# A diffusion backbone layer on one core: token pieces, paired modulation weights and a fixed TensorE order in the front

## The chip, the cores and the metric

The kernel runs on one core of a Trainium2 chip. The metric is the device time of one launch in microseconds (us), the median of three runs. A core has five engines that run side by side, each in its own order: TensorE (PE in the profile; PEld are its weight loads), VectorE (DVE), ScalarE (ACT), GpSimd (POOL) and SyncE (SP), which here issues nearly all transfers. SBUF is the memory that the engines work in, PSUM the eight banks that TensorE writes.

## The reference

One layer over 1024 latent tokens with 256 context tokens, width 1024. Cut to what matters here:

```python
mod_x = (jax.nn.silu(c) @ w_ada[i] + b_ada[i])[:, None, :]     # latent: six vectors of 1024
mod_c = jax.nn.silu(c_ctx) @ w_ada[i] + b_ada[i]               # context
sh1, sc1, g1, sh2, sc2, g2 = jnp.split(mod_x, 6, axis=-1)
csh1, csc1, ...            = jnp.split(mod_c, 6, axis=-1)
px = modulate(rms_norm(x, norm1_w[i]), sh1, sc1) @ w_in[i]     # modulate(h, s, c) = h * (1 + c) + s
pc = modulate(rms_norm(ctx, norm1_w[i]), csh1, csc1) @ w_in[i]
...  # columns of px, pc: gated DeltaNet (q, k, v with a short conv, z) and neighbourhood attention (q, k, v)
x = x + g1 * (concatenate([dn_x, na_x]) @ w_out[i])
x = x + g2 * swiglu(modulate(rms_norm(x, norm2_w[i]), sh2, sc2), w_ffn_in[i], w_ffn_out[i])
```

## The kernel before, in words

Everything is transposed: the width lies on the 128 partitions in eight tiles (`KT` = 8, index k), the 1280 tokens (256 of context, then 1024 latent) on the columns. `SEGS` cuts the columns into 256, 512 and 512, one PSUM bank each. For accuracy, each operand of a large product is split into a high part in fp32r and the rest: tokens into `hh` and `hl`, weights into `whi` and `wlo`, and a product is three: hh by whi, hh by wlo, hl by whi.

The front does this in order. The eight token tiles `xt` are loaded whole, then four of the eight tiles of the first modulation weights (`wada`), the raw weights of the first two blocks (`fraw`), and the other four. ACT squares each token tile, DVE adds the squares (`acc`), PE multiplies by ones (`m`), ACT takes a logarithm and an exponential: `rs`, the reciprocal norm of each token. `ada(q)` computes a fourth of the modulation: 16 products of weight tiles with the two conditioning vectors (`pm<-wada,wide`), a copy to the row `arow`, and four products that turn the row into columns (`pm<-sel,arow`), from which `mod1` (shift and scale) and `w1s` (norm weight times 1 + scale) are made. For each k, DVE scales `xt` by `w1s` and `rs`, ACT adds the shift and rounds (`hh`), DVE takes the rest (`hl`), and PE does the products of the first two blocks (`first`, key columns of the DeltaNet), six of the eight PSUM banks.

Behind that, one block of 128 output columns follows the other; a block's weights are cast by ACT and POOL (`load` in `weights`) into one of two buffers `whi`/`wlo`. The third block's weights are loaded early into the one raw buffer `wraw`, and cast when the buffer of the first block is free. DVE evacuates a block from PSUM while taking the taps of the convolution (`cacc`). A later job of another kind (`Wide`) has weight tiles of its own, `zhi` and `zlo`, in the pool `zp`.

What sets the order: the program is written as below, and a scheduler that simulates the engines puts the instructions of each engine in order, so products of different k and parts of `ada` can change places. Tiles wait for the last reader of the memory that they reuse.

Of the kernel before, what the change touches and what calls it, by code (L numbers as in the profile page):

```python
# [9 lines left out]
F32 = mybir.dt.float32  # L10
# [77 lines left out]
def hybrid(ctx, tc, a, dbg):  # L88
    nc = tc.nc
    pe, act, dve, pool, sp = nc.tensor, nc.scalar, nc.vector, nc.gpsimd, nc.sync  # L90
# [97 lines left out]
    def weights(wp, raws=2):  # L188
        def load(src, kt=KT, n=128, lo_engine=pool, raw=None):
# [3 lines left out]
            hi = wp.tile([128, KT, 128], F32R, name="whi", tag="whi")  # L193
            lo = wp.tile([128, KT, 128], F32R, name="wlo", tag="wlo")
# [159 lines left out]
    with ExitStack() as bs:  # L354
# [31 lines left out]
        class Block:  # L386
# [7 lines left out]
            def prefetch(self, raw=None):  # L394
# [3 lines left out]
                self.w = load_w(src, raw=raw)  # L398
# [205 lines left out]
        with ExitStack() as xs:  # L604
# [13 lines left out]
            for k in range(KT):  # L618
                x = xp.tile([128, T], F32, name=f"xt{k}", tag=f"xt{k}")
                sp.dma_start(x, a["xcT"][k])  # L620
                xt.append(x)
            for j in range(4):
                load_ada(j)
            raws = [xp.tile([128, KT, 128], F32, name=f"fraw{i}", tag=f"fraw{i}") for i in range(2)]
            for i in range(2):
                sp.dma_start(raws[i], a["w_conv"][4 + i])
            for j in range(4, 8):
                load_ada(j)
# [8 lines left out]
            def ada(q):  # L637
# [8 lines left out]
                (act.copy if q else dve.tensor_copy)(row, p)  # L646
                p = bank("pm")
                for b in range(4):
                    pe.matmul(p[:, 2 * b:2 * b + 2], row[:, b * 128:(b + 1) * 128], sel, start=True, stop=True)
                b0 = 4 * (q // 2) + 8 * (1 - q % 2)  # L650
                if q % 2:
                    for b in range(4):
                        act.activation(mod1[:, b0 + b], p[:, 2 * b:2 * b + 2], AF.Identity,
                                       bias=bada[:, b0 + b:b0 + b + 1])
                else:
                    dve.tensor_tensor(mod1[:, b0:b0 + 4], p[:, 0:8].rearrange("p (b c) -> p b c", c=2),
                                      bada[:, b0:b0 + 4].rearrange("p (b c) -> p b c", c=1).to_broadcast([128, 4, 2]),
                                      OP.add)
                    b = b0 - 8
                    dve.scalar_tensor_tensor(w1s[:, b:b + 4], mod1[:, b0:b0 + 4], 1.0,  # L660
# [3 lines left out]
            for k in range(KT):  # L664
                sq = xp.tile([128, T], F32, name="sq", tag="sq", bufs=2)
                act.activation(sq if k else acc, xt[k], AF.Square)
                if k:
                    dve.tensor_tensor(acc, acc, sq, OP.add)
# [9 lines left out]
            for k in range(KT):  # L678
# [11 lines left out]
                for b in first:  # L690
                    b.mm([k], (0, 2), 1)
# [1009 lines left out]
```

## Time and profile before

| what | us |
|---|---|
| median of three runs | 1558.21 |
| runs, lowest to highest | 1553.05 to 1559.2 |
| profiled execution | 1560.1 |
| its span in the trace | 1558.3 |
| PE busy in the span | 1469.4 (94%) |
| DVE busy | 1002.2 (64%) |
| ACT busy | 715.9 (46%) |
| POOL busy | 189.7 (12%) |

Times of the trace count from the span's start. A timeline row gives the start, the time from the first instruction's start to the last one's end, engine, line, operation, output and inputs, shape, count, and in brackets the idle time of the engine before it with what ended it. A group row gives total busy time and the mean in ns. In the view of stretches each row gives the busy time of PE, PEld, DVE, ACT and POOL in one stretch, then the granted clock of TensorE (1.00 is full), the share of the transfer engines and GB/s.

### The profile page before, as it was taken

How to read it: one execution, taken by the hardware profiler on the slowest of the kernel's cores; microseconds unless marked ns; L12 is line 12 of the kernel's file. 1: busy time of each engine (PE TensorE's matmuls, PEld its weight loads, DVE VectorE, ACT ScalarE, POOL GpSimd, SP SyncE). 2: the span in 40 equal slices, each digit the busy share in tenths (PEclk: the TensorE clock that was granted, in tenths of full speed). 3: DMA queues.
4: the chain of work that ended last, by engine and by line, in shares of the span. 5: the costliest groups of instructions: out<-in, count | busy, mean ns of one | idle time of the engine just before them, and what ended most of it. 6: DMA issues, size and time to landing. Idle time of an engine off the chain costs nothing.

```text
span 1558.3 us, 23894 instructions
## 1 busy us (share of the span) xinstructions
PE 1469.4 (94%) x8535; PEld 1226.4 (79%) x8535; DVE 1002.2 (64%) x1905; ACT 715.9 (46%) x1404; POOL 189.7 (12%) x255
## 2 busy tenths in 40 slices
PE   3999998999999989998898989999999999999998
PEld 1789777777978868887777878888888888888887
DVE  4866479345264665778886479755555656689652
ACT  5333362594356446556663175333333334444441
POOL 1043610342143300000110000000000000000000
PEclk9999999999999999999999999999999999999999
DMA  9457123554478489998627603523332234698742
GB/s 368 135 165 246 58 74 120 205 178 142 147 220 253 143 249 287 281 260 239 204 77 262 217 34 108 183 102 102 102 102 101 102 102 150 233 375 295 236 155 81
DMA packets 208455, 276.30 MB, mean 177 GB/s; under 512 B 16128, under 2 KB 115024, under 8 KB 207312
## 3 DMA queue, kind: packets, MB, share of 16 engines
q1 hardware_dynamic: 207472, 274.15, 54.7%
q8 instruction: 67, 1.10, 0.3%
q10 hardware_dynamic: 864, 0.63, 0.1%
q14 instruction: 52, 0.43, 0.1%
HBM read 209.93 MB, written 68.98 MB: 179 GB/s over the span
## 4 chain that ended last, share of the span: by engine, by line
PE 48%; DVE 2%; ACT 1%; DMA 0%; issue 0%; SPq 0%; ACTq 0%; DVEq 0%
PE ps L1267 27%; PE ps L1620 13%; PE ps L1404 3%; PE ps L1426 1%; PE sc L318 1%; PE sc L308 1%; PE sc L1210 1%; PE sc L1386 0%; DMA wraw<-w_out 0%; DVE x L1459 0%; PE ps L1134 0%; DVE bt L298 0%; PE sc L296 0%; PE ps L1103 0%; PE ps L1113 0%; PE ps L1122 0%
## 5 line engine op out<-in xcount | busy, mean ns | idle before, releaser
L383 PE MATMUL blk<-hh,whi 128*128 128x512 f32 (+1 forms) x416 | 126.8, 400 | 9.7 <-ACT zt L585 5.6
L1328 ACT CAST uhi<-ws 128x512 fp32r<-128x512 f32 x91 | 54.7, 622 | 150.5 <-PE ps L1267 71.7
L1328 ACT CAST uhi<-wq 128x512 fp32r<-128x512 f32 x101 | 60.6, 621 | 134.3 <-issue 58.0
L383 PE MATMUL blk<-hh,wlo 128*128 128x512 f32 (+1 forms) x416 | 119.7, 384 | 2.3 <-POOL wlo L199 2.3
L383 PE MATMUL blk<-hl,whi 128*128 128x512 f32 (+1 forms) x416 | 116.6, 379 | 0.0
L1329 DVE TENSOR_TENSOR ulo<-wq,uhi 128x512 fp32r<-128x512 f32 x101 | 67.4, 687 | 67.4 <-ACT uhi L1328 37.2
L1267 PE MATMUL ps<-hT,uhi 128*128 128x512 f32 x336 | 104.1, 391 | 3.1 <-ACT hT L1452 3.1
L1267 PE MATMUL ps<-lT,uhi 128*128 128x512 f32 x336 | 103.9, 391 | 0.0
L1267 PE MATMUL ps<-hT,ulo 128*128 128x512 f32 x336 | 103.6, 389 | 0.0
L383 PEld LDWEIGHTS blk<-hh,whi 128*128 128x128 f32 x416 | 71.5, 198 | 25.9 <-ACT zt L585 6.0
L383 PEld LDWEIGHTS blk<-hh,wlo 128*128 128x128 f32 x416 | 75.8, 199 | 19.4 <-POOL wlo L199 2.8
L1267 PE MATMUL ps<-hB,uhi 128*128 128x512 f32 x288 | 89.7, 392 | 0.0
L1267 PE MATMUL ps<-lB,uhi 128*128 128x512 f32 x288 | 89.2, 391 | 0.0
L1267 PE MATMUL ps<-hB,ulo 128*128 128x512 f32 x288 | 88.9, 389 | 0.0
L383 PEld LDWEIGHTS blk<-hl,whi 128*128 128x128 f32 x416 | 74.4, 194 | 14.1
L574 PE MATMUL blk<-zhi,hh 128*128 128x264 f32 (+1 forms) x288 | 85.4, 296 | 0.0
L1329 DVE TENSOR_TENSOR ulo<-ws,uhi 128x512 fp32r<-128x512 f32 x91 | 60.8, 686 | 36.4 <-ACT uhi L1328 28.1
L574 PE MATMUL blk<-zhi,hl 128*128 128x264 f32 (+1 forms) x288 | 82.8, 287 | 0.0
L574 PE MATMUL blk<-zlo,hh 128*128 128x264 f32 (+1 forms) x288 | 82.4, 286 | 0.0
L1267 PEld LDWEIGHTS ps<-hT,uhi 128*128 128x128 f32 x336 | 62.9, 188 | 16.6 <-ACT hT L1452 3.5
L1267 PEld LDWEIGHTS ps<-hT,ulo 128*128 128x128 f32 x336 | 63.3, 189 | 13.2
L1267 PEld LDWEIGHTS ps<-lT,uhi 128*128 128x128 f32 x336 | 63.4, 189 | 13.2
(341 smaller groups left out, 3539.3 us busy)
## 6 DMA issues: line engine op xcount, KB each, us to landing
wq<-w_fo SPq DMA_DIRECT2D x99, 256.0 KB
wq<-w_gu SPq DMA_DIRECT2D x88, 256.0 KB
wad<-wa SPq DMA_DIRECT2D x64, 256.0 KB
bt<-rpb SPq DMA_DIRECT2D x64, 192.0 KB
t_d<-g SPq DMA_DIRECT2D x22, 512.0 KB
fr<-t_d SPq DMA_DIRECT2D x44, 256.0 KB
f_d<-g SPq DMA_DIRECT2D x33, 256.0 KB
fr<-f_d SPq DMA_DIRECT2D x33, 256.0 KB
```

Of the source, the lines that this page charges most:

```text
L308: pe.transpose(sc[:, u * 640 + j * 128:u * 640 + (j + 1) * 128], bt[:, j * 128:(j + 1) * 128], ident)
L318: pe.matmul(sc[u * ND:u * ND + ND, 1280:1408], vv, pt[:, j * 128:(j + 1) * 128], start=j == 0, stop=j == 4)
L383: pe.matmul(o, ww[:, k], xx[k][:, s], start=k == 0 and j == 0, stop=k == KT - 1 and j == end)
L574: pe.matmul(p[:, :c1 - c0], x[k][:, s], ww[:, k, c0:c1], start=k == 0 and j == 0, stop=k == KT - 1 and j == 2)
L1210: pe.matmul(o, w[wi][:, k], parts[xi][4 + k][:, t], start=k == 0 and j == 0, stop=False, skip_group_check=True)
L1267: pe.matmul(o, w[wi][:, k], x[xi][:, k], start=first and k == 0 and j == 0, stop=k == n - 1 and j == 2, skip_group_check=True)
L1328: act.copy(hi, self.raw[key])
L1329: dve.tensor_tensor(lo, self.raw[key], hi.bitcast(F32), OP.subtract)
L1404: pe.matmul(o, w[wi][:, k], parts[xi][k][:, s], start=k == 0 and j == 0, stop=k == KT - 1 and j == 2)
L1426: pe.matmul(o, w[wi][:, k], parts[xi][k][:, s], start=k == 0 and j == 0, stop=k == KT - 1 and j == 2)
L1620: pe.matmul(o[b], w[wi][:, b], F[xn, p][xi], start=n in (0, 1, 5) and p == 0 and j == 0, stop=p == NFB // 2 - 1 and j == 2, skip_group_che ...
```

## The change

Tokens are loaded and normalised in two pieces, the first 768 columns (context and 512 latent tokens) and the last 512. The first modulation weights are ordered anew on the host, so that two of the eight tiles give scale and shift for two k: `ada` becomes a generator with two steps, run four times. The plan of the first two blocks' products is a list, in which a step `high` scales and casts one k for some columns and does hh by whi and hh by wlo, `low` does hl by whi, and a number q runs the next step of `ada(q)`; while it runs, the instructions of TensorE are kept in written order. All six PSUM banks of the two blocks are taken at the start. The third block's weights go into `zhi` and `zlo` (first 128 of 264 columns), and its cast is written ahead of the first block's evacuation.

```diff
+    class Tensor:
+        pinned = False
+        def matmul(self, *args, **kw):
+            i = nc.tensor.matmul(*args, **kw)
+            return tc.keep_in_program_order(i) if self.pinned else i
...
+    pe = Tensor()
...
-        def load(src, kt=KT, n=128, lo_engine=pool, raw=None):
+        def load(src, kt=KT, n=128, lo_engine=pool, raw=None, keep=None):
...
+            if keep:
+                hi, lo = (keep.tile([128, KT, 264], F32R, name=n, tag=n)[:, :, :128] for n in ("zhi", "zlo"))
+            else:
...
-            for k in range(KT):
-                x = xp.tile([128, T], F32, name=f"xt{k}", tag=f"xt{k}")
-                sp.dma_start(x, a["xcT"][k])
-                xt.append(x)
-            for j in range(4):
-                load_ada(j)
+            FRONT = slice(0, CT + 512), slice(CT + 512, T)
+            def load_x(s):
+                for k in range(KT):
+                    sp.dma_start(xt[k][:, s], a["xcT"][k, :, s])
...
+            load_x(FRONT[0])
+            load_ada(0)
+            load_ada(1)
             for i in range(2):
                 sp.dma_start(raws[i], a["w_conv"][4 + i])
+            load_ada(2)
+            load_ada(3)
+            load_x(FRONT[1])
             for j in range(4, 8):
                 load_ada(j)
...
                 (act.copy if q else dve.tensor_copy)(row, p)
+                yield
                 p = bank("pm")
                 for b in range(4):
                     pe.matmul(p[:, 2 * b:2 * b + 2], row[:, b * 128:(b + 1) * 128], sel, start=True, stop=True)
...
+                for b0, s in ((8 + 2 * q, p[:, 0:4]), (2 * q, p[:, 4:8])):
+                    dve.tensor_tensor(mod1[:, b0:b0 + 2], s.rearrange("p (b c) -> p b c", c=2), col(bada, b0), OP.add)
+                dve.scalar_tensor_tensor(w1s[:, 2 * q:2 * q + 2], mod1[:, 8 + 2 * q:10 + 2 * q], 1.0, col(n1w, 2 * q),
+                                         op0=OP.add, op1=OP.mult)
+                yield
+            def token_norms(segs):
+                s0, s1 = segs[0][0], sum(segs[-1])
+                for k in range(KT):
+                    sq = xp.tile([128, CT + 512], F32, name="sq", tag="sq", bufs=3)[:, :s1 - s0] if k else acc[:, s0:s1]
+                    act.activation(sq, xt[k][:, s0:s1], AF.Square)
+                    if k:
+                        dve.tensor_tensor(acc[:, s0:s1], acc[:, s0:s1], sq, OP.add)
+                for t0, n in segs:
+                    p = bank()
+                    pe.matmul(p[:, :n], M[C_ONE], acc[:, t0:t0 + n], start=True, stop=True)
+                    act.activation(rs[:, t0:t0 + n], p[:, :n], AF.Ln, bias=b_eps, scale=1.0 / D)
+                act.activation(rs[:, s0:s1], rs[:, s0:s1], AF.Exp, scale=-0.5)
...
+            s0, s1, ALL = SEGS[:2], SEGS[2:], SEGS
...
+            high, low = (lambda k, s: (normed(k, s), products(k, (0, 2), s))), (lambda k, s: products(k, (1,), s))
+            plan = [(0,), (0,), (high, 0, s0), (high, 1, s0), (1,), (low, 0, s0), (low, 1, s0), (1,), (high, 2, s0),
+                    (high, 3, s0), (2,), (low, 2, s0), (low, 3, s0), (token_norms, s1), (high, 0, s1), (2,), (high, 1, s1),
+                    (low, 0, s1), (low, 1, s1), (high, 2, s1), (3,), (high, 3, s1), (low, 2, s1), (low, 3, s1), (3,),
+                    (room,), (high, 4, ALL), (high, 5, ALL), (low, 4, ALL), (high, 6, ALL), (low, 5, ALL),
+                    (high, 7, ALL), (low, 6, ALL), (low, 7, ALL)]
...
+        jobs[2].prefetch(keep=zp())
         first[0].evac()
-        jobs[2].prefetch()
...
-    o["wa1"] = c(wada[:, :2048].reshape(8, 128, 4, 512).transpose(2, 1, 0, 3)[[2, 0, 3, 1]])
+    o["wa1"] = c(wada[:, :2048].reshape(8, 128, 2, 4, 256).transpose(3, 1, 0, 2, 4)[:, :, :, ::-1].reshape(4, 128, 8, 512))
```

Three places of the order. First TensorE, where the modulation for further k is made (the numbers behind `hh` and `hl` name buffers: 133 and 134 are k 0, 135 and 136 k 1, 137 and 138 k 2, 139 and 140 k 3). Before, around the third part of `ada`:

```order
L643 MATMUL pm<-wada,wide 32x512 x8
L383 MATMUL blk<-hh_137,whi 128x256
L383 MATMUL blk<-hh_137,whi 128x512 x2
L383 MATMUL blk<-hh_137,wlo 128x256
L649 MATMUL pm<-sel,arow 128x2 x4
L643 MATMUL pm<-wada,wide 32x512 x4
L383 MATMUL blk<-hh_137,wlo 128x512 x2
```

Now, around the second run of `ada` (rows that stand twice, once for each block, are shown once, here and in the next place):

```order
L98 MATMUL pm<-wada,wide 32x512 x8
L98 MATMUL blk<-hl_134,whi 128x256
L98 MATMUL blk<-hl_134,whi 128x512
L98 MATMUL blk<-hl_136,whi 128x256
L98 MATMUL blk<-hl_136,whi 128x512
L98 MATMUL pm<-sel,arow 128x2 x4
L98 MATMUL blk<-hh_137,whi 128x256
L98 MATMUL blk<-hh_137,whi 128x512
```

Before, the four `sel` products stood among products of the same k 2, which did not need them; now they stand right ahead of k 2, which does.

Second, TensorE at the norm of the tokens' second piece (before, all three `m` products stood at the program's start):

```order
L98 MATMUL blk<-hl_140,whi 128x256
L98 MATMUL blk<-hl_140,whi 128x512
L98 MATMUL m<-acc,ones 128x512
L98 MATMUL blk<-hh_133,whi 128x512
L98 MATMUL blk<-hh_133,wlo 128x512
L98 MATMUL pm<-sel,arow 128x2 x4
```

The product `m` of the second piece stands behind four k of the first piece, and directly behind it the first product that needs its result.

Third, ScalarE at the end of the first two blocks. Before:

```order
L686 ACTIVATE hh_417<-xt_164,mod_103 128x1024
L416 ACTIVATE cacc<-blk,cw 128x256
L416 ACTIVATE cacc<-blk,cw 128x512 x2
L198 CAST whi<-wraw 128x1024
L416 ACTIVATE cacc<-blk,cw 128x256
```

Now:

```order
L705 ACTIVATE hh_465<-xt_157,mod_103 128x1024
L216 CAST zhi<-wraw 128x8x128
L434 ACTIVATE cacc<-blk,cw 128x256
L434 ACTIVATE cacc<-blk,cw 128x512 x2
L216 CAST whi<-wraw 128x1024
```

The cast of the third block's weights has moved from behind the first block's evacuation (`cacc`) to ahead of it, right behind the last `hh`.

94 lines of the change are left out of this document (43 added, 51 removed).

## The prediction

> **What bounds the kernel now.** I read the page's busy line and slices first, then the stretches of the front one clock period at a time, then the timeline of the first 99 us, engine by engine.
>
> ```profile
> PE 1469.4 (94%) x8535; PEld 1226.4 (79%) x8535; DVE 1002.2 (64%) x1905; ACT 715.9 (46%) x1404; POOL 189.7 (12%) x255
> PE   3999998999999989998898989999999999999998
> ```
>
> PE is busy in nearly every slice but the first. Behind the third block the instructions of PE stand in the same order in both kernels, so a microsecond won or lost before it should arrive at the end whole. The question is when PE finishes its first three blocks.
>
> Stretches (columns: PE, PEld, DVE, ACT, POOL busy us, granted clock, DMA share, GB/s):
>
> ```profile
> 23.31:26.72 3.41, 3.23 (x5) 1.85 (x6) 0.13 (x1) 0.73 (x2) 0.00 (x0) 1.00 1.01 420
> 33.55:36.96 3.41, 1.44 (x9) 1.15 (x9) 3.41 (x3) 3.21 (x9) 2.24 (x1) 0.99 1.02 423
> 36.96:40.37 3.41, 2.96 (x7) 2.28 (x8) 3.41 (x2) 2.81 (x4) 2.74 (x2) 0.50 1.02 423
> 40.37:43.79 3.42, 3.42 (x11) 2.74 (x11) 3.42 (x5) 2.70 (x3) 0.00 (x0) 0.51 0.85 270
> 74.51:77.92 3.41, 1.38 (x6) 0.60 (x4) 3.41 (x7) 3.41 (x6) 1.38 (x1) 0.99 0.61 196
> 77.92:81.33 3.41, 2.37 (x8) 2.08 (x9) 3.41 (x7) 0.08 (x1) 0.99 (x1) 0.50 0.21 60
> 81.33:84.75 3.42, 3.42 (x10) 2.74 (x10) 3.42 (x7) 1.62 (x2) 0.50 (x1) 0.51 0.31 93
> ```
>
> The granted clock moves in periods of 3.41 us. A period in which PE is busy about 40% (1.44 and 1.38 of 3.41) is followed by half clock; half clock ends only behind a period that is busy throughout (3.42), not behind 2.96 or 2.37. So one stall of PE costs its own length and up to two periods at half clock, some 3 us of lost work. This happens twice in the front: before the first products and between the second and third block.
>
> The first chain (ACT, PE and DVE; start, duration):
>
> ```profile
> 12.67 1.27 ACT L666 ACTIVATE sq<-xt 128x1280 f32<-128x1280 f32 x1 [0.95 <-DMA xt<-xcT]
> 20.46 1.27 ACT L666 ACTIVATE sq<-xt 128x1280 f32<-128x1280 f32 x1 [0.29 <-DMA xt<-xcT]
> 23.49 3.98 PE L671 MATMUL m<-acc,ones 128*128 128x256 f32 x6 [23.49 <-DVE acc L668]
> 26.46 0.69 ACT L672 ACTIVATE rs<-m,bias 128x512 f32<-128x512 f32 x1 [1.23 <-PE m L671]
> 27.51 0.69 ACT L672 ACTIVATE rs<-m,bias 128x512 f32<-128x512 f32 x1 [0.36 <-PE m L671]
> 28.21 1.28 ACT L673 ACT_TABLE_LOAD   x1
> 29.51 1.27 ACT L673 ACTIVATE rs<-rs 128x1280 f32<-128x1280 f32 x1
> 27.40 1.92 PE L643 MATMUL pm<-wada,wide 128*32 128x512 f32 x16
> 29.39 0.69 DVE L646 COPY arow<-pm 128x512 f32<-128x512 f32 x1 [5.95 <-PE pm L643]
> 30.14 1.05 PE L649 MATMUL pm<-sel,arow 128*128 128x2 f32 x8 [0.81 <-DVE arow L646]
> 31.23 0.17 DVE L656 TENSOR_TENSOR mod<-pm,prm 128x8 f32<-128x8 f32 x1 [1.15 <-PE pm L649]
> 31.70 10.68 DVE L685 SCALAR_TENSOR_TENSOR xt<-xt,w1s,rs 128x256 f32<-128x256 f32 x8
> 36.01 0.39 PE L383 MATMUL blk<-hh,whi 128*128 128x256 f32 x1 [1.21 <-ACT hh L686]
> ```
>
> Tokens arrive until 20.46, the norms are ready at 30.8, the modulation at 31.7, and the products start at 36.01. From there PE has next to no gaps until 74.92:
>
> ```profile
> 46.38 1.92 PE L643 MATMUL pm<-wada,wide 128*32 128x512 f32 x16
> 48.23 0.85 PE L383 MATMUL blk<-hh,whi 128*128 128x256 f32 x3
> 54.52 0.95 PE L649 MATMUL pm<-sel,arow 128*128 128x2 f32 x8
> 59.50 0.75 PE L383 MATMUL blk<-hh,whi 128*128 128x256 f32 x3
> 63.02 0.28 PE L383 MATMUL blk<-hh,whi 128*128 128x256 f32 x1
> 72.41 2.51 PE L383 MATMUL blk<-hl,whi 128*128 128x256 f32 x12
> 76.52 0.62 PE L383 MATMUL blk<-hh,whi 128*128 128x256 f32 x2 [1.60 <-ACT whi L198]
> 78.96 1.01 PE L383 MATMUL blk<-hh,wlo 128*128 128x256 f32 x2 [1.48 <-POOL wlo L199]
> ```
>
> One k of both blocks takes 3.52 us (59.50 to 63.02), a modulation part 1.85 us (46.38 to 48.23), its second step 0.95. Of the 38.9 us, eight k are 28.2, two modulation parts with their second steps 5.6, half clock (36.96 to 43.79) some 3.4; the rest, 1.7, is waiting at the start.
>
> **The change, part by part.**
>
> *Tokens in pieces.* Prices of arrival, two stretches and the group of the adds:
>
> ```profile
> 2.00:8.00 6.00, 0.00 (x0) 0.00 (x0) 0.00 (x0) 2.77 (x3) 0.20 (x1) 1.00 0.76 219
> 8.00:20.00 12.00, 0.00 (x0) 0.00 (x0) 7.38 (x6) 7.46 (x6) 1.18 (x1) 1.00 1.03 421
> L668 DVE TENSOR_TENSOR acc<-acc,sq 128x1280 f32<-128x1280 f32 x7 | 10.4, 1492 | 2.6 <-ACT sq L666 2.1
> ```
>
> At 12.67 three tiles of 640 KB were in, as much as five of the new 384 KB pieces; three more at 421 GB/s take 2.8 us, so piece one is complete at 15.5 instead of 20.46. A square and an add of 768 columns (0.6 of 1.27 and of 1.492) bring its norm product to 17.3. Two such products took 2.97 us (23.49 to 26.46): 20.3. That was near half speed, since the third, of 512 columns, took 1.05 (to 27.51); the clock column shows 1.00 until the first change. Then 0.69, table 1.28, exponential about 0.8: norms at 23.1, 7.7 us earlier.
>
> *First modulation weights by pairs of tiles.* The two weight tiles that k 0 and 1 need (2.1 MB) land 5 us behind piece one, at 20.5, so they end the chain now. The 16 instructions took 1.99 us until the copy (27.40 to 29.39) with the clock just up; here PE has been busy for only 3 us, no whole period, and is still slow: 1.9 or 3.8, I take 3.5. Copy 0.69, second step 1.1 to 1.8, three DVE steps of about 0.2 (one more than before; four ACT steps are gone), a scaling and a cast of 256 columns 0.9, five hand-overs of about 0.1: the first product starts at 28.2, between 26.1 (full clock) and 28.5. That is 7.8 us won.
>
> *Two more modulation parts, norms and fixed order behind the start.* PE now issues behind its start three modulation parts (5.6) with second steps (2.9), and the second piece's norm product (1.05, from 26.46 to 27.51), beside the same 28.2: 28.2 + 37.8 = 66.0 without any wait. PE keeps its written order, and in two places nothing lies between a result and its user. Prices for the chain there:
>
> ```profile
> L688 DVE SCALAR_TENSOR_TENSOR hl<-xt,mod,hh 128x1024 fp32r<-128x1024 f32 x8 | 10.2, 1273 | 0.0
> L688 DVE SCALAR_TENSOR_TENSOR hl<-xt,mod,hh 128x256 fp32r<-128x256 f32 x8 | 3.8, 475 | 0.9 <-ACT hh L686 0.9
> L686 ACT ACTIVATE hh<-xt,mod 128x256 fp32r<-128x256 f32 x8 | 4.1, 514 | 0.0
> ```
>
> Behind the second step for k 2 and 3 the next instruction of PE needs three DVE steps (0.6), an add that DVE has between them (about 0.6), a scaling (0.475) and a cast (0.514): 2.2 us; its 512 columns come 1.1 later, because ACT has a square between. Behind the norm product of piece two stands its first user: logarithm 0.69, table 1.28, exponential 0.6, scaling and cast of 512 columns (between the rows of 256 and 1024) 0.75 and 0.73: 4.05 us. The kernel before had such steps too, but PE had products of another k to do meanwhile. At the start the cast of the second block's weights stands before the 512-column cast and costs about 1.4. Stalls together 8.8: 74.8.
>
> Clock: 2.7 lost at the start (two periods at half, less the wait inside them). Each of the two long stalls leaves a period about 40% busy, or two of about 50%, depending on where the periods lie; the first drops the clock, the second perhaps not. From 3.1 for each I take one and a half: 4.7. End of the second block: 82.2, against 74.92: 7.3 lost.
>
> [...]
>
> DVE gets 23 instructions more, ACT seven, two table loads among them. DVE's work behind the start is 28.0 as before (eight k of 2 x 1.273 and 2 x 0.475), about 1.6 for eight more short pieces, 4.3 for seven adds and 1.8 for nine small steps: 36 us, from 27 to 63. PE's 82 covers it, and 19 us of slack are its cover; only if PE lost nothing would DVE be close behind it. So beyond the stalls I cost them at nothing. The eight added token issues on SP stand behind four weight tiles; bytes are the same, so the last tiles land as before at about 44, and PE wants them at 48 or later.
>
> *Third block's weights in free buffers.* Before, cast and subtraction waited for the second block's end:
>
> ```profile
> 73.90 1.63 ACT L416 ACTIVATE cacc<-blk,cw 128x256 f32<-128x256 f32 x3 [11.93 <-PE blk L383]
> 76.54 2.37 POOL L199 TENSOR_TENSOR wlo<-wraw,whi 128x1024 fp32r<-128x1024 f32 x1 [36.84 <-ACT whi L198]
> 75.47 12.68 DVE L425 SCALAR_TENSOR_TENSOR cacc<-blk,cw,cacc 128x255 f32<-128x255 f32 x22
> ```
>
> The waits were 1.60 and 1.48, and 77.92 to 84.75 at half clock, with 1.04 idle in it, costs 2.9: 6.0 together. Now the cast follows ACT's last hh, about 5 us before PE is done, and 1.05 + 2.37 fit. What is late next is a PSUM bank: PE can do eleven pairs (3.9 us) with the two free ones, while the first bank is freed by six DVE steps of 0.58 and one of 0.74, 4.2 us. So 5.7 of the 6.0 is won. The buffers are those of the first wide job, whose weights can be cast only behind the third block now; two casts, two POOL steps, a load and POOL's other work of that time are an estimated 14 us, against the fourth block's eight k of 1.76 (14.1) and its transposes, some 17 in all: nothing, with 3 us to spare.
>
> Sum: 7.3 - 5.7 = 1.6 us slower. On the profiled execution (1560.1, span 1558.3) that gives 1561.7; the median of the runs shown is 1558.2, hence 1559.8.
>
> **Rivals.**
>
> *The stalls do not come.* If the two waits are covered after all and the clock stays up behind them, the second block ends at 66.0 + 1.4 + 2.7 = 70.1, 4.8 earlier; with the third block 10.5 won: 1548. For it: PE had no gap from 40 to 74 before. Against: the rows of the order. It decides once stalls and clock together lose less than 7 of the 16.2 us; all stalls, but the clock up throughout, are 1552.
>
> *Short token rows move slowly.* Piece one has rows of 3072 bytes instead of 5120. If they moved at the 219 GB/s of the stretch from 2 to 8, 3.15 MB take 14.4 us instead of 7.5, and everything behind moves by 6.9: 1567. From 230 GB/s down it is over 0.5% slower. Against: that stretch carries small constants too, and from 8 us on the queues are full at 421.
>
> *The third block gains nothing,* if its weights' memory comes free only with the last token tile: 1566. Against: it lies where the first two token tiles were, last read long before.
>
> **How the numbers follow.** About 0.5% (8 us) is what a measurement here can tell from none. My forecast, with bounds of two throttles and late weights on one side and none on the other (-5 to +6), has 0.68; stalls covered 0.17 (nearly all of it faster); slow rows 0.07; third block without gain 0.08, half of it slower. So faster 0.16, same 0.73, slower 0.11. The forecast's own range is 1553 to 1566; 1549 to 1567 leaves out most of the two extreme cases.
>
> **What would show it.** First products at 28 and norms at 23 confirm the start. Gaps on PE of about 2 and 4 us, before hh of k 2 and before the second piece's first hh, with half clock behind them, confirm the loss. The last hl product should end near 82, and the third block follow with no wait over 0.5 us at full clock. I am wrong if PE has no gap over 1 us between 30 and 75, or if tokens land later than 17.

## The result, and the profile after

The changed kernel takes 1567.45 us (median of four runs, 1567.09 to 1570.22), the kernel before on the same chip 1555.96: a ratio of 1.0075, with a 95% interval of 1.0056 to 1.0093. That is 11.5 us slower, where 1.6 were forecast, and just above the upper end of the range. The profiled execution took 1567.09 (span 1565.3). That of the kernel before, at 1560.1, was 3.6 over the median of 28 later runs (1556.5), so the two traces account for 7.0 of the 11.5.

The busy line and the slices of the page:

```profile
PE 1474.1 (94%) x8535; PEld 1228.9 (79%) x8535; DVE 1008.9 (64%) x1928; ACT 719.9 (46%) x1411; POOL 190.3 (12%) x255
PE   4899988999999989998898989999999999999998
```

The first slice holds more work of TensorE than before (4 tenths against 3), the second less (8 against 9: both stalls lie in it); where the rest went this line does not show. The front, from the timeline of ScalarE and TensorE (start, duration, what ended the wait):

```profile
22.41 0.84 ACT L695 ACTIVATE rs<-rs 128x768 f32<-128x768 f32 x1
27.81 0.58 PE L98 MATMUL blk<-hh,whi 128*128 128x256 f32 x1 [2.21 <-ACT hh L705]
40.78 0.58 PE L98 MATMUL blk<-hh,whi 128*128 128x256 f32 x1 [1.99 <-ACT hh L705]
41.91 0.80 PE L98 MATMUL blk<-hh,whi 128*128 128x512 f32 x1 [0.55 <-ACT hh L705]
55.82 0.80 PE L98 MATMUL blk<-hh,whi 128*128 128x512 f32 x1 [4.26 <-ACT hh L705]
81.14 2.51 PE L98 MATMUL blk<-hl,whi 128*128 128x256 f32 x12
83.49 0.51 PE L98 MATMUL blk<-hh,zhi 128*128 128x256 f32 x2
```

Norms at 23.25, first product at 27.81 (36.01 before), the two long waits in the two places foreseen, the last hl group at 81.14, and the third block behind it with no wait. Stretches of one clock period (columns as before: PE, PEld, DVE, ACT, POOL busy, granted clock, DMA share, GB/s):

```profile
36.96:40.37 3.41, 1.83 (x14) 1.61 (x13) 2.23 (x7) 2.33 (x6) 0.00 (x0) 1.00 1.02 423
40.37:43.79 3.42, 2.46 (x7) 1.89 (x7) 3.42 (x7) 2.62 (x5) 0.00 (x0) 0.51 1.03 343
43.79:47.20 3.41, 3.41 (x15) 2.59 (x17) 3.13 (x6) 1.26 (x2) 0.00 (x0) 0.50 0.04 9
50.61:54.03 3.42, 0.95 (x3) 0.12 (x1) 0.00 (x0) 2.85 (x4) 0.00 (x0) 1.00 0.00 0
54.03:57.44 3.41, 1.62 (x4) 1.34 (x5) 2.74 (x4) 2.24 (x4) 0.00 (x0) 0.51 0.00 0
57.44:60.85 3.41, 3.41 (x14) 3.03 (x13) 1.42 (x5) 0.00 (x0) 0.00 (x0) 0.50 0.00 0
60.85:64.27 3.42, 3.42 (x10) 2.48 (x8) 3.42 (x6) 0.72 (x1) 0.00 (x0) 0.50 0.00 0
```

Behind both stalls the granted clock stood at half, 0.51 and 0.50 for two periods behind the first (the stretch ahead of them was busy 1.83 of 3.41), 0.51, 0.50 and 0.50 for three behind the second: the stretch from 57.44 was busy throughout, and the next one was still at 0.50. The second block's last products end at 83.65 (81.14 + 2.51) against 74.92, 8.7 us late where 7.3 were worked out; the third block wins 6.2 of it back, and the wide job begins at 118.05 against 115.55: 2.5 us late. In these two traces the forecast held up to here; other executions will show that part of this is luck.

What it missed comes behind. TensorE in the wide job, first the kernel before, then the changed one:

```profile
156.31 1.02 PE L218 MATMUL m<-ones,acc 128*128 128x1 f32 x8 [1.77 <-DVE modp L220]
```
```profile
127.83 0.39 PE L98 MATMUL blk<-zhi,hh 128*128 128x264 f32 x1 [1.95 <-DVE cacc L443]
163.94 1.84 PE L98 MATMUL m<-ones,acc 128*128 128x1 f32 x8 [3.39 <-DVE modp L238]
```

A wait for a PSUM bank that the fourth block's taps (`cacc`) still read is new; with the half clock behind it (0.51 from 129.13 to 132.54) the lag is 6.0 us. A wait in front of the products that sum up the second modulation (`m<-ones,acc`) has doubled, and the lag is 8.0 at ScalarE's first exponential behind the wide job (`EG<-m`, 178.38 against 170.40). Both wait for VectorE. Its steps `acc<-wad` (one weight tile of the second modulation each) and the fourth block's taps, in the kernel before:

```profile
64.23 0.47 DVE L231 TENSOR_SCALAR acc<-wad,sc 128x512 f32<-128x512 f32 x1
65.92 2.33 DVE L233 SCALAR_TENSOR_TENSOR acc<-wad,sc,acc 128x512 f32<-128x512 f32 x3 [1.22 <-DMA wad<-wa]
69.11 2.33 DVE L233 SCALAR_TENSOR_TENSOR acc<-wad,sc,acc 128x512 f32<-128x512 f32 x3 [0.86 <-DMA wad<-wa]
71.87 0.75 DVE L233 SCALAR_TENSOR_TENSOR acc<-wad,sc,acc 128x512 f32<-128x512 f32 x1 [0.44 <-DMA wad<-wa]
120.32 6.51 DVE L425 SCALAR_TENSOR_TENSOR cacc<-blk,cw,cacc 128x254 f32<-128x254 f32 x11 [5.64 <-ACT cacc L416]
152.99 3.17 DVE L233 SCALAR_TENSOR_TENSOR acc<-wad,sc,acc 128x512 f32<-128x512 f32 x4 [6.40 <-DMA wad<-wa]
```

and in the changed one:

```profile
78.76 0.48 DVE L249 TENSOR_SCALAR acc<-wad,sc 128x512 f32<-128x512 f32 x1
80.12 1.92 DVE L251 SCALAR_TENSOR_TENSOR acc<-wad,sc,acc 128x512 f32<-128x512 f32 x1 [0.89 <-DMA wad<-wa]
110.55 2.46 DVE L249 TENSOR_SCALAR acc<-wad,sc 128x512 f32<-128x512 f32 x1
113.59 2.31 DVE L251 SCALAR_TENSOR_TENSOR acc<-wad,sc,acc 128x512 f32<-128x512 f32 x3
117.55 7.75 DVE L251 SCALAR_TENSOR_TENSOR acc<-wad,sc,acc 128x512 f32<-128x512 f32 x4 [1.65 <-DMA wad<-wa]
125.23 6.49 DVE L443 SCALAR_TENSOR_TENSOR cacc<-blk,cw,cacc 128x254 f32<-128x254 f32 x11
158.09 3.11 DVE L251 SCALAR_TENSOR_TENSOR acc<-wad,sc,acc 128x512 f32<-128x512 f32 x4 [8.08 <-DMA wad<-wa]
```

Before, VectorE was through with the front at 64.2 and did nine of these steps (the eight shown and one at 72.75) ahead of the first block's taps, while TensorE still had 10.7 us of front products to go. Now it ends the front at 78.8, 4.9 us ahead of TensorE, and does two. In both kernels sixteen stand ahead of the fourth block's taps. Seven have lost their place: from 110.55 on there are now eight, where one stood before (at 111.75). They fill the gap in which VectorE waited for ScalarE before (5.64 us), run slowly there (2.46 us for the first and 7.75 for the last four, against 2.31 for the three between), and the taps start at 125.23 instead of 120.32. At the second wait VectorE itself lacks weight tiles: a buffer for the next tile comes free only when a step is done, and it is further behind. At 152.99 the kernel before had four steps left, at 158.09 the changed one has six.

### The profile page after: what moved, and what is told of

The parts are those of the page before. It is cut to its first block, busy times and chain, and to the rows that moved or that the text cites. A ratio compares the mean times of both kernels' runs of the same rounds, so it can differ in the third digit from the quotient of the medians.

```text
span 1565.3 us, 23927 instructions
## 1 busy us (share of the span) xinstructions
PE 1474.1 (94%) x8535; PEld 1228.9 (79%) x8535; DVE 1008.9 (64%) x1928; ACT 719.9 (46%) x1411; POOL 190.3 (12%) x255
## 4 chain that ended last, share of the span: by engine, by line
PE 48%; DVE 2%; ACT 1%; DMA 0%; issue 0%; SPq 0%; ACTq 0%; DVEq 0%
PE ps L98 45%; PE sc L98 2%; PE sc L102 1%; DMA wraw<-w_out 0%; DVE x L1504 0%; DVE bt L316 0%; ACT pt L329 0%; DVE lB L1498 0%; ACT x L1505 0%; DVE s L1190 0%; ACT L1408 0%; DVE bt L321 0%; DVE x L1417 0%; DVE oacc L1212 0%; DVE gal L1221 0%
## 5 line engine op out<-in xcount | busy, mean ns | idle before, releaser
L98 PE MATMUL ps<-hT,uhi 128*128 128x512 f32 x496 | 147.0, 391 | 3.1 <-ACT hT L1497 3.1
L98 PE MATMUL ps<-lT,uhi 128*128 128x512 f32 x496 | 146.6, 390 | 0.0
L98 PE MATMUL ps<-hT,ulo 128*128 128x512 f32 x496 | 146.3, 389 | 0.0
L98 PE MATMUL ps<-hB,uhi 128*128 128x512 f32 x436 | 129.8, 391 | 0.0
L98 PE MATMUL ps<-lB,uhi 128*128 128x512 f32 x436 | 129.3, 390 | 0.0
L98 PE MATMUL ps<-hB,ulo 128*128 128x512 f32 x436 | 128.9, 389 | 0.0
L98 PEld LDWEIGHTS ps<-hT,uhi 128*128 128x128 f32 x496 | 93.0, 188 | 22.7 <-ACT hT L1497 3.5
L98 PEld LDWEIGHTS ps<-hB,uhi 128*128 128x128 f32 x436 | 82.2, 188 | 17.5 <-issue 0.5
L98 PEld LDWEIGHTS ps<-lB,uhi 128*128 128x128 f32 x436 | 82.1, 188 | 17.1
L98 PEld LDWEIGHTS ps<-hB,ulo 128*128 128x128 f32 x436 | 81.9, 188 | 16.9
L98 PEld LDWEIGHTS blk<-hh,whi 128*128 128x128 f32 x392 | 69.0, 200 | 32.2 <-ACT hh L705 11.8
```

The source lines that it names most:

```text
L98: i = nc.tensor.matmul(*args, **kw)
```

## The experiments

The theory, **backlog**: what the forecast missed is some seven steps of the second modulation (the expectations say eight), pushed from under the front's products to ahead of the taps. Rivals: **weights** (the wide job's weights come late, since the third block sits in their buffers), **phase** (where the clock's periods happen to fall), and **front** (the stalls cost more than the trace of the front shows). Every kernel below had five rounds beside the kernel before (the changed one its four runs). The marks are from the profiled executions (us): the wide job's first product, `EG<-m`, the first product of the feed-forward stage (`ps<-hB`), and the span.

| kernel | wide | EG | hB | span | ratio to before (95%) |
|---|---|---|---|---|---|
| before | 115.55 | 170.40 | 911.49 | 1558.3 | 1 |
| after | 118.05 | 178.38 | 918.49 | 1565.3 | 1.0075 (1.0056 to 1.0093) |
| b_pin | 112.99 | 179.00 | 918.41 | 1565.4 | 1.0076 (1.0059 to 1.0093) |
| a_fewer | 120.10 | 174.50 | 917.25 | 1563.9 | 1.0024 (1.0011 to 1.0038) |
| b_keep | 109.86 | 165.29 | 907.08 | 1555.1 | 0.9981 (0.9969 to 0.9993) |
| a_nokeep | 125.11 | 186.27 | 924.29 | 1572.1 | 1.0099 (1.0079 to 1.0119) |
| a_fill | 110.65 | 171.16 | 911.92 | 1558.9 | 1.0035 (1.0024 to 1.0045) |
| a_spare | 117.60 | 186.86 | 925.90 | 1573.8 | 1.0119 (1.0097 to 1.0141) |
| g_fill_spare | 111.97 | 182.60 | 918.07 | 1566.4 | 1.0066 (1.0046 to 1.0086) |
| g_fill2_spare | 108.11 | 176.44 | 910.47 | 1558.4 | 1.0041 (1.0028 to 1.0054) |
| b_keep3 | 110.20 | 172.73 | 915.57 | 1563.5 | 1.0017 (1.0003 to 1.0032) |
| a_half | 118.38 | 170.26 | 917.05 | 1562.8 | 1.0045 (1.0025 to 1.0065) |
| b_half | 110.13 | 166.91 | 905.33 | 1552.1 | 0.9994 (0.9982 to 1.0005) |
| g_half | 110.20 | 162.09 | 903.85 | 1550.7 | 0.9994 (0.9975 to 1.0012) |
| g2_half | 109.40 | 161.31 | 903.37 | 1550.1 | 0.9972 (0.9957 to 0.9987) |
| a_tail | 118.74 | 172.17 | 907.06 | 1555.7 | 1.0007 (0.9991 to 1.0023) |
| b_tail | 113.73 | 163.30 | 901.22 | 1548.4 | 0.9966 (0.9952 to 0.9980) |
| bk_tail | 109.25 | 163.98 | 902.02 | 1550.9 | 0.9961 (0.9947 to 0.9975) |
| g2_tail | 108.03 | 159.80 | 894.76 | 1542.0 | 0.9929 (0.9902 to 0.9956) |
| the same again | 108.78 | 160.67 | 898.36 | 1548.5 | 0.9950 (0.9935 to 0.9965) |

**The backlog alone, in the kernel before.** In `modulation`, both forms of the step become

```diff
-                    dve.scalar_tensor_tensor(acc2, x, sc, acc2, op0=OP.mult, op1=OP.add)
+                    i = dve.scalar_tensor_tensor(acc2, x, sc, acc2, op0=OP.mult, op1=OP.add)
+                if len(qs) == 4:
+                    tc.keep_in_program_order(i)
```

> The kernel before, with the 32 steps of the second modulation on VectorE held behind everything written before them on that engine, so that none runs in the front beside TensorE's products; nothing else is touched and no work is added. Theory 'backlog': the eight steps that ran at 64 to 74 us move behind the taps, the fourth block's taps start several us later, a wait on cacc appears on TensorE in the wide job near 123 us, and the time rises by 3 to 6 us, to 1559 to 1562. Rivals 'weights' and 'phase': no change, 1556 within 1.5 us.

TensorE in it:

```profile
126.82 0.59 PE L576 MATMUL blk<-zhi,hh 128*128 128x264 f32 x1 [4.83 <-DVE cacc L427]
164.91 1.83 PE L218 MATMUL m<-ones,acc 128*128 128x1 f32 x8 [4.35 <-DVE modp L220]
```

The front is the old one, no work is added, the wide job even begins 2.6 us earlier, and the kernel is as slow as the changed one. The same two waits stand there. The price was set at half of what it is, since only the first wait was counted. That the two totals agree is chance: here all nine steps lose their place, all 32 are held in written order, and the loss in this trace is 11.2 us from the wide job to `EG`, against 5.5 in the changed kernel.

Why the wide job begins earlier: two products of the third block now stand ahead of its wait for `wlo`, which is 1.03 instead of 1.48 us, and the clock stayed up behind the third block's waits, where the kernel before had 0.50 in the second of these stretches and 0.51 in the next. In b_pin:

```profile
74.51:77.92 3.41, 1.81 (x8) 0.93 (x7) 3.34 (x7) 3.41 (x6) 1.33 (x1) 1.00 0.00 0
77.92:81.33 3.41, 2.38 (x13) 2.00 (x13) 3.41 (x7) 0.12 (x1) 1.05 (x1) 1.00 0.27 83
```

What hangs on the clock alone shows b_tail, a kernel further down. Up to the wide job its TensorE order is that of the kernel before, product for product, and its waits at the third block are the same 1.60 and 1.48:

```profile
77.92:81.33 3.41, 3.15 (x10) 2.67 (x11) 3.41 (x7) 0.00 (x0) 0.21 (x1) 0.61 0.49 142
81.33:84.75 3.42, 3.42 (x17) 2.84 (x16) 3.42 (x7) 2.44 (x3) 1.34 (x1) 0.89 0.04 12
```

There the clock was at half from 37.7 to 41.1 and from 78.7 to 82.1, in the kernel before for twice as long each time (36.96 to 43.79, 77.92 to 84.75), and the wide job begins at 113.73 instead of 115.55. So *phase* is worth some 1.8 us in this front, from one execution to another, an estimate from these two.

**Fewer steps in the changed kernel.**

```diff
-        order = [(q, k) for q in qs for k in range(KT)]
+        order = [(q, k) for q in qs for k in range(KT) if q or not k]
```

(with the loop skipping the same seven steps; their loads are left out too.)

> The changed kernel with seven of the 32 steps of the second modulation left out: its first quarter loads and uses only the first of its eight weight tiles, so four columns of modp are not the reference's. Theory 'backlog' (VectorE ends the front 14.5 us later than before, so eight of these steps, which ran beside TensorE's last front products at 64 to 74 us before, now stand ahead of the fourth block's taps): with seven steps fewer the taps start near 121 us instead of 125.2, the wait of 2.0 us on cacc near 128 us and the half clock behind it go, and the time falls by 3 to 6 us, to 1562 to 1564. Rival 'weights' (the wide job's weights, whose buffers the third block now borrows, come late) and rival 'phase' (where the clock's periods fall): the wait stays, 1567 within 1.5 us.

VectorE and TensorE in it:

```profile
122.86 6.51 DVE L448 SCALAR_TENSOR_TENSOR cacc<-blk,cw,cacc 128x254 f32<-128x254 f32 x11 [5.24 <-ACT cacc L439]
160.64 1.02 PE L98 MATMUL m<-ones,acc 128*128 128x1 f32 x8 [1.81 <-DVE modp L238]
```

VectorE waits for ScalarE again ahead of the taps, the wait on `cacc` is gone, and the later one is back at 1.8. This execution's front was 2.1 us later than the changed kernel's and its `EG` still 3.9 earlier. The median fell by 0.5% of 1556 us, 7.9: more than expected. *Weights* and *phase* fall with these two runs as explanations of the two waits: b_pin borrows no buffers and adds both waits, a_fewer keeps the buffers borrowed and loses them.

**The third part, alone and left out.** b_keep is the kernel before with `prefetch(keep=zp())` ahead of the first evacuation; a_nokeep the changed kernel without it.

> The kernel before, with only the third part of the change: the third block's weights in the wide job's free buffers and cast ahead of the first evacuation. The prediction's 5.7 us: the waits of 1.60 and 1.48 us and the half clock from 78 to 85 us go, 1550 within 1.5. Theory 'backlog' agrees, since VectorE's front is untouched and 5.6 us of idle time stand ahead of the fourth block's taps. Rival 'weights': what is won is lost again at the start of the wide job, 1555 or more.

> The changed kernel without its third part: the third block's weights in their own buffers again, cast behind the first evacuation. By the prediction's sum it loses 5.7 us: a ratio of 1.011. Theory 'backlog': VectorE's late steps stand in the same places, and the third block's wait gives VectorE up to 6 us of time to catch up, so the waits of 2.0 and 3.4 us shrink and the loss is smaller: 1.008 to 1.010.

The first waits of each kernel behind the second block:

```profile
79.18 0.47 PE L386 MATMUL blk<-hh,zhi 128*128 128x512 f32 x1 [0.79 <-DVE cacc L428]
```
```profile
138.99 0.59 PE L98 MATMUL blk<-zhi,hh 128*128 128x264 f32 x1 [5.73 <-DVE cacc L443]
```

In b_keep the wide job begins 5.69 us earlier, the prediction's 5.7, with the bank wait of 0.79 that it named; 4.4 of them are left at the feed-forward stage and 3.2 in the span; over all runs the gain is 3.0 (1.1 to 4.8), less than the 5.7 worked out. In a_nokeep the bank wait grew to 5.73 instead of shrinking, which backlog as I had it did not foresee; the third part is worth 0.24% there, 3.7 us, give or take 4.

**The order of TensorE's front.**

```diff
-            plan = [(0,), (0,), (high, 0, s0), (high, 1, s0), (1,), (low, 0, s0), (low, 1, s0), (1,), (high, 2, s0),
-                    (high, 3, s0), (2,), (low, 2, s0), (low, 3, s0), (token_norms, s1), (high, 0, s1), (2,), (high, 1, s1),
+            plan = [(0,), (0,), (high, 0, s0), (1,), (high, 1, s0), (1,), (low, 0, s0), (low, 1, s0), (high, 2, s0),
+                    (high, 3, s0), (token_norms, s1), (2,), (low, 2, s0), (low, 3, s0), (2,), (high, 0, s1), (high, 1, s1),
```

> The changed kernel with the hand-written order of TensorE's front changed so that work stands in both waits: the second modulation part right behind the products of k 0 and its second step ahead of the hl products, the norm product of the second piece ahead of the third modulation part, and that part's second step ahead of the second piece. Same instructions, other order. Stalls as the loss (2.5 and 4.3 us, and the half clock behind them, 3 and 4.8): the waits before hh of k 2 and of the second piece fall below 1 us each, the second block ends near 72 to 75 us instead of 83.5, and the time falls by 8 to 11 us, to 1557 to 1560. If the half clock comes whatever the order, 1561 to 1563. If VectorE is close behind TensorE (its own front needs 36 us of work), new waits on its results take the place of the old ones and the time stays above 1563.

TensorE in it:

```profile
46.47 1.46 PE L98 MATMUL m<-acc,ones 128*128 128x512 f32 x2 [2.93 <-DVE acc L690]
120.93 0.39 PE L98 MATMUL blk<-zhi,hh 128*128 128x264 f32 x1 [2.45 <-DVE cacc L443]
```

The wait before the second piece is gone and that before k 2 is down to 0.49 and 0.75, a new one of 2.93 stands before the norm product (VectorE's adds are late), and the third block starts at 76.09 instead of 83.49. Of these 7.4 us 0.40% of 1556, 6.2, is left over all runs. The wait on `cacc` ends 6.9 us earlier but did not shrink: VectorE's front ends 7.4 earlier too (71.36), still 4.9 ahead of TensorE's, and again only two steps fit in. So the front's loss and the backlog are two losses.

**The steps moved within the stage.** None with the fourth block, three instead of two with each tile of the wide job, held behind the taps:

```diff
-                    bg2.step(1)
+                    bg2.step(int(n < 3))
...
-                    bg2.step(2)
+                    bg2.step(3)
```

> The changed kernel with the front untouched and the second modulation's steps moved: none is issued with the fourth block, three instead of two with each tile of the wide job, and each stays behind what was written before it on VectorE. Same work, same results. Theory 'backlog': only eight steps then stand ahead of the fourth block's taps, which start as soon as ScalarE has begun the evacuation (about 119 us); the wait of 2.0 us on cacc and the half clock behind it go, and the time falls by 4 to 8 us, to 1559 to 1563, most of what leaving out seven steps gave (1559.6). If 24 steps in the wide job end later than the 16 there now, the wait of 3.4 us near 160 us grows and eats it: 1565 or more. Rival 'phase': 1567 within 1.5.

> Both mends together: TensorE's front in the order that fills the two waits, and the second modulation's steps moved out of the fourth block. If the front's loss and the backlog are two losses, the gains add: 5.5 from the order and 4 to 8 from the steps, 1554 to 1558, level with the kernel before. If they are one loss seen twice: no better than the better of the two, 1560 to 1562.

> As the one before, with the norm product of the second piece later in TensorE's order (behind the hl products of k 2 and 3, where the sum that it reads is ready) and the fourth modulation part behind it as cover. The wait of 2.9 us for acc at 46 us should go and one of about 1.2 us for the second piece's hh come instead; the second block ends 1 to 3 us earlier than with the first order, and the time is 1552 to 1557. If VectorE's front work (36 us from 27 us on, with its own waits) is now the bound, the end of the second block does not move.

> The kernel before with the third block's weights in free buffers, and three steps of the second modulation instead of two with each tile of the wide job. The wait of 1.3 to 1.8 us for the last of these steps near 150 us, behind which the clock is halved for a period or two, goes if the steps end earlier: 2 to 4 us under the version without it, 1548 to 1550. If what ends them is when their weight tiles land, nothing moves: 1552.

TensorE in a_spare, then in b_keep3:

```profile
133.16 1.84 PE L98 MATMUL m<-ones,acc 128*128 128x1 f32 x8 [5.13 <-DVE acc L251]
172.22 1.17 PE L98 MATMUL m<-ones,acc 128*128 128x1 f32 x8 [4.60 <-DVE acc L251]
```
```profile
148.56 1.62 PE L221 MATMUL m<-ones,acc 128*128 128x1 f32 x7 [7.65 <-DVE acc L236]
```

All four missed their forecasts; of a_spare the second branch came, that the later wait grows and eats the gain. The wait on `cacc` went, as it should, but TensorE's summing products stand at fixed places in its order, and where VectorE's sums come later than that place, or the place moves earlier (b_keep3), TensorE stands 4 to 8 us. Another place in the same stage did not help; whether the stage has too many of these steps is what the next kernels ask. g_fill2_spare, with the norm product later, begins the wide job 3.9 us ahead of g_fill_spare, so that order is the better one.

**Half of the steps in another stage.** Quarters 2 and 3 are read by the feed-forward stage only:

```diff
-        bg2.add(modulation(pools(bg2s, "adp", "left"), range(4), bank))
+        bg2.add(modulation(pools(bg2s, "adp", "left"), range(2), bank))
...
-        late.add(modulation(pools(os_, "adp", "left"), range(4, 6), bank))
+        late.add(modulation(pools(os_, "adp", "left"), range(2, 6), bank))
```

with two `late.step()` for one in the output projection, and the first eight steps held to the third block, the next eight to the wide job (not held in b_half).

> The changed kernel, its front untouched, with half of the second modulation (quarters 2 and 3, whose results are read only by the feed-forward stage) moved to the output projection, where two steps are done at a time instead of one. Of the 16 steps that stay, eight run with the third block and eight with the wide job, behind the fourth block's taps; TensorE's products that read their sums come some tiles later. The moved steps in the run before this traded the wait on cacc for waits of 5.1 and 4.6 us on those products; theory 'backlog' says that VectorE and the transfers have 16 steps too many in this stage, so with half of them gone both the wait at 128 us and that at 160 us go: 8 to 11 us less, 1557 to 1561 on a chip where the kernel before takes 1557. Rival: the waits only move to the output projection, 1565 or more.

> The kernel before with the third block's weights in free buffers, and half of the second modulation moved to the output projection in the same way. Only the wait of 1.3 to 1.8 us near 150 us and the half clock behind it are to be won here: 1.5 to 4 us under the version with the weights alone (ratio 0.998), so a ratio of 0.995 to 0.997. Rival as above: the output projection loses as much.

> TensorE's front in the order that fills the two waits (second block's end at 76 us) and half of the second modulation moved. Front and backlog as two separate losses: 5.5 us from the order and 8 to 11 from the steps, a ratio to the kernel before of 0.994 to 0.998. If the gain of the order is lost again to VectorE's taps, the ratio is above 1.000.

> As the one before, with the norm product of the second piece later and the fourth modulation part behind it; in the earlier pair this ended the second block 4 us earlier (73.6 against 77.5 us). A ratio 0.002 below the one before: 0.992 to 0.996, and level with or below the kernel before with the third part alone and half the steps moved.

All four came out 0.1 to 0.25% above their forecasts.

a_half at the end of the output projection: a wait of TensorE, then the stretch (columns as above), and last the same stretch of the kernel before:

```profile
890.15 1.55 PE L98 MATMUL ps<-ones,acc 128*128 128x1 f32 x8 [2.38 <-DVE acc L251]
```
```profile
890.00:900.00 10.00, 9.85 (x33) 8.12 (x34) 3.42 (x7) 1.83 (x3) 0.00 (x0) 0.66 0.66 227
```
```profile
890.00:900.00 10.00, 10.00 (x46) 8.26 (x45) 2.26 (x5) 0.28 (x1) 0.00 (x0) 1.00 0.14 53
```

By `EG` the 8.0 us of the changed kernel's lag are gone (170.26), both waits with them, though a wait of 2.05 for the wide job's weights has come (taken up below). By `hB` the kernel is 5.6 behind the one before again, because the moved steps were drained ahead of the last pair of blocks, with another late sum and a granted clock of 0.66 in the stretch from 890 to 900. The stretch behind, where transfers stood at 0.14, was the better place.

**The moved half ending with the last pair.** `late.step(2)` goes into the loop of the last pair, and `late.drain()` with the step for `w2s` behind it.

> The changed kernel with its front untouched and quarters 2 and 3 of the second modulation moved as in the kernel before this one, but ending with the last pair of the output projection (where the transfers stood at 0.15 of the engines' time and VectorE had 2.3 of 10 us busy) instead of being drained ahead of it. Theory 'backlog' as the whole excess: what remains over the kernel before is the front's own loss, 2 to 4 us, a ratio of 1.001 to 1.003. If the output projection still loses: 1.0045 as before. If something else in the changed kernel costs: above 1.005.

> The kernel before with half of the second modulation moved to the last pair of the output projection, as in the changed kernel's version that came out at a ratio of 1.0007; all else as before. What is to be won here is the wait of 1.77 us near 156 us and one period at half clock behind it: 0 to 4 us, a ratio of 0.9975 to 1.000. Then the front's own loss is the difference of the two versions, 1 to 5 us, as the traces have it (2.5 us at the end of the fourth block). If the kernel before won 8 us or more from it, the steps were no special burden of the change.

> The kernel before with the third part and with the moved half: what can be had without the new front. b_keep gave 0.998; with 0 to 4 us more 0.9955 to 0.998.

> The best of the kernels so far (the front's order with both waits filled, half of the second modulation moved) with the moved half ending with the last pair of the output projection. The first profile won 14.2 us by 840 us and lost 6.1 of them there; if the new place is idle, most of the 6 comes back: a ratio of 0.992 to 0.995, under both kernels and under the kernel before with the third part alone (0.998). If not: 0.997.

> The best kernel so far once more (new front with both waits filled, third part, moved half), beside the version without the new front: 0.993 again, within 0.0025. If the new front is worth its 7 us of earlier start once nothing waits behind it, this stays 3 to 7 us under that version.

The changed kernel then stands at 1.0007, level with the one before. But the kernel before wins 0.34% (5.3 us) by the same move (without the hold, as in b_half), more than expected, so of the change's 0.75% the steps are not all: 0.41%, some 6.4 us with an uncertainty of about 3, is left between a_tail and b_tail. The traces show where. The wide job begins 5.0 us later in a_tail than in b_tail, and then waits for its weights. TensorE in a_tail, and SyncE's queue in it; under them the load of these weights in the changed kernel:

```profile
121.29 0.39 PE L98 MATMUL blk<-zlo,hh 128*128 128x264 f32 x1 [2.04 <-POOL zlo L587]
104.17 4.75 SPq L230 DMA_DIRECT2D wad<-wa  x3
111.54 0.58 SPq L568 DMA_DIRECT2D kk_d<-kk  x1
112.16 0.77 SPq L585 DMA_DIRECT2D wraw<-w_nv  x1
```
```profile
102.80 0.33 SPq L583 DMA_DIRECT2D wraw<-w_nv  x1
```

The tiles of held-back steps have four buffers; three loads wait on SyncE until VectorE frees one (to 108.92), then a store waits for its data, `kk` (to 111.54), and the wide job's weights stand behind both, 9.4 us later than in the changed kernel, where they stand ahead of these. Rival *weights* is no part of the changed kernel's loss (no wait at 118.05), but a few places of the queue away from it.

With both waits of the front filled, the third part and the moved half, g2_tail takes 0.9929 and, in a second run of five rounds, 0.9950 (0.9935 to 0.9965) of the kernel before: the fastest of all, and clearly under the changed kernel. Beside bk_tail, which has the old front and no hold (0.9961), the second measurement is not separated. So what the new front is worth by itself, with nothing waiting behind it, stays between nothing and 5 us.

## Why the prediction was wrong, point by point

- *The start.* First product at 28.2 worked out, 27.81 measured; norms 23.1 and 23.25. Right, including the 16 instructions ahead of the first copy (3.42 against 3.5 taken, where 16 such took 1.92 at 34.48). The pieces of 3072 bytes arrived at 414 GB/s from 8 to 15 us, against 421 for the longer rows: that rival is out.
- *The stalls.* Worked out 2.2, 1.1 and 4.05; measured 1.99, 0.55 and 4.26. Right in place and size. The rival in which they do not come is out.
- *The clock.* Taken at one and a half throttles behind the start, 4.7 us; there were two, over five periods, whose 14.3 us of work at granted clocks of 0.50 and 0.51 cost an estimated 7.2, half of it. The first gap was 1.99 us, and two periods at 0.51 and 0.50 followed it. What the prediction read from the rows of the kernel before is too simple: 57.44 to 60.85 was busy throughout and the next stretch still stood at 0.50, and behind 1.81 of 3.41 (74.51 to 77.92) in b_pin the next stood at 1.00, where behind 1.83 in the changed kernel it stood at 0.51. The earlier start and the shorter stalls gave 1 us of these 2.5 back, so the second block ended at 83.65 against 82.2.
- *The third part.* 5.7 worked out. In single traces it came out so: 6.2 in the changed kernel, 5.7 in the kernel before, each at the fourth block's end. Over all runs b_keep gained 3.0 (1.1 to 4.8), so the term was too large. Its 2.9 of half clock were read from one execution; in b_tail the same two waits cost one period instead of two. And b_keep's trace had one period at half at the start (38.4 to 41.8), where the kernel before had two, which the third part does not explain.
- *The step that failed* is VectorE's: "36 us, from 27 to 63. PE's 82 covers it, and 19 us of slack are its cover ... So beyond the stalls I cost them at nothing." The 36 us of work were about right (34.3 busy from 27 to 78.76), but the sum left out 17.5 us of VectorE's own waits, 6.59 of them for `rs` and 4.44 for a square, and it ended at 78.8, not 63. And the slack was not empty: in the kernel before, the steps `acc<-wad` at 64.23 to 72.75 stood in it, in a timeline that I had read. I asked what covers VectorE's front, and not what VectorE did next and who waits for that. Losing their place cost 3.5 us at the fourth block's taps and 2.0 at the sums. That it can by itself make a kernel this slow is shown by b_pin: 11.8 us (9.2 to 14.5) with nine of them moved and no other work added. No rival of the prediction had this; its range reached up only for throttles and late weights.
- *"A microsecond won or lost before it should arrive at the end whole."* A pair of traces can't show it: the two executions of g2_tail are 0.9 us apart at `EG` and 6.5 at the end, so what lies behind wanders. b_keep's 5.7 arrived as 3.0, and g2_half's 9.1 at `EG` as 8.2 in its span and 4.4 over all runs; the last step is mostly the height of the one profiled execution of before.
- *The base.* The sum stood on a median of three runs, 1558.2; 17 to 31 runs gave 1556.5 to 1558.4, so up to 2 us of the miss are the base's.

How the 11 us divide is settled only roughly. In the two traces 2.5 us are front and 5.5 are waits for VectorE: 8.0 at `EG`, of which 7.0 are left at the end. The rest is the height of the one profiled execution of before over its median (3.6) and that of the changed kernel's median over its profiled execution (0.4). Part of it has a place: with the old front and without the third part the wide job begins at 115.55 and 113.73 (before, b_tail), with the changed front and the third part at 117.60 to 120.10 (the changed kernel, a_fewer, a_spare, a_half and a_tail). The means, 114.6 and 118.6, put the front's loss nearer 4 us than 2.5, an estimate from seven executions. With the 5.5 behind it that makes between 9 and 10 of the 11.

## What to carry to other kernels

When an engine finishes a stage earlier than the engine that bounds it, look at what it does in that time before calling it slack: here it was another stage's work, and making VectorE late moved that work to where TensorE waits for it. A background task should be put where its engine, its transfers and the queue that issues them are all idle, and the products that read its result must stand in the bounding engine's order behind the latest time at which it can be done; moving the steps without the readers only moved the wait. Take a cause away in the kernel before as well as in the changed one: a_tail without b_tail would have credited nearly the whole 11 us to it.

## What the hardware showed

VectorE's steps `acc<-wad` took 0.77 us each (2.31 for three at 113.59) while GpSimd did nothing, and 1.94 each (7.75 for four at 117.55) beside GpSimd:

```profile
110.26 2.47 POOL L585 TENSOR_TENSOR zlo<-wraw,zhi 128x1056 fp32r<-128x1056 f32 x1
117.94 2.63 POOL L217 TENSOR_TENSOR wlo<-wraw,whi 128x1024 fp32r<-128x1024 f32 x1 [5.21 <-ACT whi L216]
120.70 3.19 POOL L558 TENSOR_TENSOR kd<-kk,cst 128x1280 f32<-128x1280 f32 x1
```

The single step at 110.55 took 2.46, as long as the GpSimd step beside it. The four took 4.7 us more than alone, of the 5.8 that GpSimd was busy; GpSimd's own step at 110.26 was no longer than the same step at 100.26 (2.51), beside which VectorE was mostly idle (1.80 us, until 102.24). The taps, which read PSUM and one SBUF tile, took 0.59 each (6.49 for eleven from 125.23), with GpSimd's copies beside them until 128.24. That GpSimd's work made these steps longer is the author's reading of these times: no experiment took that work away. The eight steps from 110.55 on took 12.5 us together, against 5.9 at the times that they have alone (0.48 and seven of 0.77).
